# Hybrid S5/HGRN2 block: output projection operands made beside the gating products, norm factors in columns, and four reorderings

## The chip, the cores and the metric

The kernel runs on one core of one Trainium2 chip. A core has TensorE (PE, with its weight loads shown as PEld), VectorE (DVE), ScalarE (ACT), GpSimd (POOL) and SyncE (SP), whose queue issues nearly all DMAs here. The metric is the device time of one execution in microseconds; the median of the runs counts.

## The reference, cut to what matters

One layer over 1024 tokens of width 1024, all in float32:

```python
h = h + 0.5 * swiglu(rmsnorm(h, ffn1_norm), w_gate, w_up, w_down)    # d_ff 2816
u = rmsnorm(h, mix_norm)
s5_in, q, f, i, g, gate_a, gate_b = split_columns(u @ w_in)
y_a = (gelu(s5(s5_in)) @ glu_val) * sigmoid(gelu(s5(s5_in)) @ glu_gate)
o = head_rmsnorm(hgrn2(q, f, i), out_norm) * silu(g)                 # 8 heads of 128
y_b = o @ hg_w_out
h = h + (sigmoid(gate_a) * y_a + sigmoid(gate_b) * y_b) @ w_merge_out
h = h + 0.5 * swiglu(rmsnorm(h, ffn2_norm), ...)
h = h + sigmoid(rmsnorm(h, ple_norm) @ ple_w_gate) * (p @ ple_w_proj)
return rmsnorm(h, final_norm)
```

## The kernel before, in words

Activations are kept transposed: 8 blocks of 128 channels, two halves (h = 0, 1) of 512 tokens, in the tile `r1` (the program's name r). Every large product is taken in three passes of fp32r: each operand is split into a high part (ScalarE, L98 for weights, L345 for activations) and a low part, a subtraction (L99, L346) on VectorE or GpSimd. `mm3` (L354) issues the three passes; a plain unit `proj` is 24 matmuls of 128x512. PSUM has eight buffers of 128x512, the temporaries `t` are eight buffers, the split weights lie in seven slots, the raw weights in four.

Larger products use a seven-product scheme: from the four quarters of the input the sums s1 to s4 are made (`operands`, L452 to L461), from the weights t1 to t4 (`begin`, L119, on VectorE), and each of the seven products is 12 matmuls. `pair` does this for two 128-column blocks of the gates (gg, ga, gb) and of the HGRN2 output projection ("out"); `strassen` does it in the ffns, for 18 of the 22 column blocks, numbers 4 to 21. The split operands lie in the quarters `q0` to `q6`.

Work that is not a matmul is put between matmuls by hand. `self.queue` and `self.scan` are lists of steps; after every fourth matmul `tick` takes one entry from each. An integer n uses up n ticks, a string is a mark that uses one. `flush` runs a queue up to a mark at once. `after(n, f)` runs f when n more `mm3` calls (or steps of the down projection) are through. Beyond that a scheduler orders each engine's instructions at build time: those that it takes to be ready go first, in order of tracing. `paced`, `issue_after` and `keep_in_program_order` add edges to it that fix an order on one engine. Each engine then runs its list in order.

The stages, with their place in the profiled span: ffn1's gate and up products (19 to 477 us), its down projection in seven products of 11 steps (477 to 689, L718), the mixer's S5 input and the first two gate blocks (689 to 757), the other gates as pairs (757 to about 1000), eight HGRN2 heads (to 1453), the S5 gating products `glu` (to 1573, with the last head's steps inside), the output projection (to 1666), the merge, ffn2, and the embedding with the final norm.

What the change touches:

- `norm_rs`: the sum over channels of the squares, by one matmul with ones (L394), then the reciprocal root as eleven VectorE operations on 128x512 (`rsqrt_mean`, L372 to L378). It is called seven times: once in ffn1, twice before the mixer, twice in the merge, twice after ffn2. The final norm (`final`, L1593 and L1605) does it in another form: columns, eleven small operations, diagonals, and matmuls that spread them.
- `s5_params` prepares the S5 parameters on VectorE in 13 pieces. `jobs` calls it (`go`) once in each block of ffn1 from block 5 on, beside its own loads and subtractions (L598) for the down projection. ffn2 has no such pieces.
- `hg_steps(j)`: a head's steps. `gate` loads the stored gate; seven levels (L1207 on TensorE) need the head's k (L1167 on VectorE); transposition, state, output and `back` follow, 34 ticks in all.
- `glu_load` and `glu_split` (L1444, L1445): the S5 output is loaded into eight temporaries and split into q2 and q3, where the mixer's input lay. The last head's f projection is done with h = 1 first so that q2 and q3 come free.
- `glu`: 16 units of 24 matmuls. `mid` runs after the thirteenth: it ends the last head, makes the operands of the output projection and queues the rest.
- `merge`: after the last pair, `mixed` splits the mixed activations, and h is reloaded (L1500) into the rows of r1 that the splits have read. The pairs' `out` loads side_gb (L1484) and the gated S5 part (L1485).

## Time and profile before

| | us |
|---|---|
| median of 3 runs (lowest, highest) | 2557.45 (2555.87, 2560.57) |
| the profiled execution's own time | 2556.42 |
| its span, first to last instruction | 2554.6 |

| engine | busy us | share |
|---|---|---|
| PE | 2449.2 | 96% |
| PEld | 2053.6 | 80% |
| DVE | 1945.9 | 76% |
| ACT | 899.5 | 35% |
| POOL | 885.4 | 35% |

The mean granted TensorE clock is 0.98 of full speed. Times in the rows are microseconds from the span's start. Busy time of PE includes the pipelined tail of each matmul, so a pause shorter than that tail is not seen as idle.

### The profile page before, as it was taken

Reading aid. Unit: us, or ns where it says so; the run is one execution under the profiler, and the core shown is the slowest. Engines: PE = TensorE matmul, PEld = TensorE weight load, DVE = VectorE, ACT = ScalarE, POOL = GpSimd, SP = SyncE. Lnnn points to the kernel's source line nnn. Section 1 sums busy time; section 2 is a strip of 40 time slices with the busy share of each in tenths; the row PEclk is TensorE's granted clock in tenths of the full one; section 3 lists DMA queues with packets and bytes.
Section 4 is the critical chain, followed back from the end, with each engine's and each line's share of the span. In section 5 each row is a group of like instructions: output and inputs, shape, how many; then the busy total and the mean of one; then the engine's idle time right before and its main releaser. Section 6 shows DMA issues by size and latency. Waiting matters only on the chain. (4 is left out here: it accounts for less than half of the span.)

```text
span 2554.6 us, 33785 instructions
## 1 busy us (share of the span) xinstructions
PE 2449.2 (96%) x12030; PEld 2053.6 (80%) x12030; DVE 1945.9 (76%) x2997; ACT 899.5 (35%) x1586; POOL 885.4 (35%) x604
## 2 busy tenths in 40 slices
PE   9999999999999999999999897989999999999996
PEld 7887777788878788989989785878888888788886
DVE  8999999657788775685785557936989999657757
ACT  4322322445534343213213323323332232445533
POOL 3345555200137454112011116652245555200153
PEclk9999999999999999999999998999999999999998
DMA  4255665867423344313312433452246655766212
GB/s 153 91 196 173 207 206 176 287 222 227 147 63 115 124 147 146 81 46 77 86 50 59 137 100 103 152 166 75 83 173 209 228 199 200 272 227 208 86 58 91
DMA packets 195369, 373.29 MB, mean 146 GB/s; under 512 B 34912, under 2 KB 49504, under 8 KB 195168
## 3 DMA queue, kind: packets, MB, share of 16 engines
q1 hardware_dynamic: 194512, 370.57, 44.2%
q8 instruction: 95, 1.56, 0.3%
q14 instruction: 74, 0.61, 0.1%
q10 hardware_dynamic: 688, 0.55, 0.1%
HBM read 257.48 MB, written 113.57 MB: 145 GB/s over the span
## 5 line engine op out<-in xcount | busy, mean ns | idle before, releaser
L354 PE MATMUL mm<-q,wsplit 128*128 128x512 f32 (+1 forms) x7452 | 1705.2, 388 | 50.4 <-ACT q L345 27.5
L354 PEld LDWEIGHTS mm<-q,wsplit 128*128 128x128 f32 x7452 | 1379.4, 190 | 347.0 <-ACT q L345 31.1
L99 POOL TENSOR_TENSOR wsplit<-wraw,wsplit 128x512 fp32r<-128x512 f32 x368 | 536.5, 1472 | 1100.3 <-PE mm L718 386.9
L718 PE MATMUL mm<-wsplit 128*128 128x512 f32 x1848 | 424.0, 392 | 7.4 <-ACT wsplit L345 4.1
L718 PEld LDWEIGHTS mm<-wsplit 128*128 128x128 f32 x1848 | 348.9, 189 | 82.1 <-ACT wsplit L345 5.0
L98 ACT ACTIVATE wsplit<-wraw 128x512 fp32r<-128x512 f32 x464 | 279.8, 624 | 375.0 <-PE mm L354 171.6
L346 DVE TENSOR_TENSOR wsplit<-space,wsplit 128x512 fp32r<-128x512 f32 x308 | 207.8, 712 | 122.7 <-PE mm L718 86.3
L345 ACT ACTIVATE wsplit<-space 128x512 fp32r<-128x512 f32 x308 | 192.4, 631 | 206.2 <-PE mm L718 165.8
L119 DVE TENSOR_TENSOR wraw<-wraw 128x512 f32<-128x512 f32 x153 | 148.0, 968 | 38.5 <-POOL wsplit L99 34.5
L545 DVE TENSOR_TENSOR t<-t,mm 128x512 f32<-128x512 f32 x252 | 167.9, 676 | 0.0
L99 POOL TENSOR_TENSOR wsplit<-t,wsplit 128x512 fp32r<-128x512 f32 x51 | 86.2, 1690 | 211.9 <-ACT wsplit L98 189.9
L598 DVE TENSOR_TENSOR r<-r 128x512 f32<-128x512 f32 x120 | 146.5, 1221 | 6.9 <-DMA r<-in_ffn_w_down_dram 6.1
L98 ACT ACTIVATE wsplit<-t 128x512 fp32r<-128x512 f32 x51 | 32.3, 632 | 266.6 <-DVE t L119 226.4
L1207 PEld LDWEIGHTS mm<-space,space 128*128 128x128 f32 x896 | 109.0, 195 | 16.0 <-DVE space L1167 6.6
L1207 PE MATMUL mm<-space,space 128*128 128x64 f32 x896 | 109.5, 275 | 11.5 <-DVE space L1167 8.8
L99 DVE TENSOR_TENSOR wsplit<-wraw,wsplit 128x512 fp32r<-128x512 f32 x96 | 114.8, 1201 | 4.1 <-ACT wsplit L98 2.6
L354 PE MATMUL mm<-wsplit,q 128*128 128x256 f32 x768 | 101.2, 286 | 0.0
L548 ACT ACTIVATE t<-t 128x512 f32<-128x512 f32 x72 | 45.5, 632 | 141.5 <-DVE t L545 141.5
L354 PEld LDWEIGHTS mm<-wsplit,q 128*128 128x128 f32 x768 | 94.4, 191 | 0.1
L515 POOL TENSOR_TENSOR a<-a 128x512 f32<-128x512 f32 x44 | 70.5, 1601 | 62.1 <-DVE a L536 42.8
L1213 DVE TENSOR_TENSOR space<-space 128x512 f32<-128x512 f32 x48 | 35.2, 734 | 71.1 <-PE mm L1207 71.1
L1334 DVE TENSOR_TENSOR t<-t,mm 128x512 f32<-128x512 f32 x105 | 69.6, 677 | 18.6 <-PE mm L354 12.1
(244 smaller groups left out, 2108.2 us busy)
## 6 DMA issues: line engine op xcount, KB each, us to landing
space<-ffn_act SPq DMA_DIRECT2D x154, 256.0 KB, 3.2
ffn_act<-a SPq DMA_DIRECT2D x110, 256.0 KB, 5.6
wraw<-in_ffn_w_gate_dram SPq DMA_DIRECT2D x44, 512.0 KB, 3.3
wraw<-in_ffn_w_up_dram SPq DMA_DIRECT2D x44, 512.0 KB, 4.2
r<-in_ffn_w_down_dram SPq DMA_DIRECT2D x22, 1024.0 KB, 6.2
ffn_sums<-r SPq DMA_DIRECT2D x22, 1024.0 KB, 6.5
wraw<-in_w_in_dram SPq DMA_DIRECT2D x44, 512.0 KB, 3.8
space<-ffn_sums SPq DMA_DIRECT2D x88, 256.0 KB, 2.8
```

The source lines that it names most:

```text
L98: self.nc.scalar.activation(hi, src, AF.Copy)
L99: engine.tensor_tensor(out=lo, in0=src, in1=hi.bitcast(F32), op=ALU.subtract)
L119: sub = lambda out, x, y: v.tensor_tensor(out=out, in0=x, in1=y, op=ALU.subtract)
L345: self.nc.scalar.activation(hi, src, AF.Copy)
L346: lo_engine.tensor_tensor(out=lo, in0=src, in1=hi.bitcast(F32), op=ALU.subtract)
L354: self.last = nc.tensor.matmul(ps, al if p == 2 else ah, bl if p == 1 else bh, start=p == order[0] and i == 0, stop=p == order[2] and i == ...
L515: g.tensor_tensor(out=x[n], in0=x[a], in1=x[b], op=op)
L545: add = lambda out, x, y: v.tensor_tensor(out=out, in0=x, in1=y, op=ALU.add)
L598: v.tensor_tensor(out=room[:, out, :], in0=room[:, x, :], in1=room[:, y, :], op=ALU.subtract)
L718: self.last = nc.tensor.matmul(ps[j], a[:, j * P:(j + 1) * P], b, start=p == 0 and m == 0, stop=p == NP - 1 and m == 2)
L1207: nc.tensor.matmul(ps[:, c * 64:(c + 1) * 64].rearrange("p (b i) -> p b i", i=h), K[:, c * HC:(c + 1) * HC], q3[:, c * cb:(c + 1) * cb, :] ...
L1334: add = lambda o, x, y: nc.vector.tensor_tensor(out=o, in0=x, in1=y, op=ALU.add)
```

## The change

- `norm_rs` multiplies the squares' sums, 128 columns at a time, with one column of ones, so that the sum over channels lies in four columns of 128 tokens (a new small tile `cols`). The eleven operations run on 128x4. One `mm3` later `spread` makes four diagonals (VectorE), multiplies them with ones (four matmuls of 128 columns) and copies the result (ScalarE). The calls after the ffns come one step earlier in two places.
- `operands` does every low part on VectorE, always uses its gap, and ends its sums with a mark. The output projection's operands are queued behind the last head's steps with gaps of three ticks (`switch`); `mid` only ends that queue and adds a12, and s4 follows the units.
- The S5 parameters: in `jobs` a piece in every second block; the others in the first two products of the down projection, at steps 2, 5 and 8.
- In the S5 matrices' scan the first wait is 30 ticks instead of 16, the waits of 5 are 4. A head waits two more ticks between its gate and its first level.
- The first pair (gg, 1) begins with t2, t3, t1 and takes b11 fourth; its product is added to three sums then.
- The last head: S5 output loaded before its projections, then q and f for h = 1, the splits, q and f for h = 0.
- The reloads of h in the merge are kept behind what is traced on SP before them.

```diff
@@ -232,6 +232,7 @@
...
         nc.vector.memset(self.ones, 1.0)
         self.rs = c.tile([P, 2, HALF], F32, name="rs")
+        self.cols = c.tile([P, 2, 3, 4], F32, name="cols")
         self.gain = {}
@@ -387,12 +388,26 @@
             nc.scalar.activation(sq, self.hsrc(j, h), AF.Square)
             (engine or nc.gpsimd).tensor_tensor(out=accs[h], in0=accs[h], in1=sq, op=ALU.add)
-    def norm_rs(self, h, acc, out=None):
+    def norm_rs(self, h, acc):
+        nc = self.nc
         ps = self.aux()
         with self.tc.issue_after(self.last.ins):
-            self.nc.tensor.matmul(ps, self.ones, acc, start=True, stop=True)
-        self.rsqrt_mean(self.rs[:, h, :], ps, D)
+            for c in range(4):
+                nc.tensor.matmul(ps[:, c:c + 1], acc[:, c * P:(c + 1) * P], self.ones[:, 0:1], start=True, stop=True)
+        cols = iter([self.cols[:, h, i, :] for i in range(3)])
+        col = next(cols)
+        self.rsqrt_mean(col, ps[:, 0:4], D, lambda: next(cols))
+        def spread():
+            ps = self.aux()
+            for c in range(4):
+                dg = self.t()[:, 0:P]
+                nc.vector.tensor_scalar(out=dg, in0=self.ident, scalar1=col[:, c:c + 1], scalar2=None, op0=ALU.mult)
+                with self.tc.issue_after(self.last.ins):
+                    nc.tensor.matmul(ps[:, c * P:(c + 1) * P], self.ones, dg, start=True, stop=True)
+            nc.scalar.activation(self.rs[:, h, :], ps, AF.Copy)
+        self.after(1, spread)
     def norm_x(self, j, h, gain):
@@ -438,7 +453,6 @@
         v = self.nc.vector
-        g = v if gain else self.nc.gpsimd
         A11, A22, A12, S4, S1, S2, S3 = roles
@@ -452,16 +466,16 @@
...
             v.tensor_tensor(out=s1, in0=x21, in1=x22, op=ALU.add)
             v.tensor_tensor(out=s2, in0=s1, in1=x11, op=ALU.subtract)
-            self.split(self.quarter(S3, k), s3, g)
+            self.split(self.quarter(S3, k), s3, v)
             if early:
...
             else:
                 self.split(self.quarter(S1, k), s1, v)
-            self.split(self.quarter(S2, k), s2, g)
+            self.split(self.quarter(S2, k), s2, v)
             v.tensor_tensor(out=s4, in0=x12, in1=s2, op=ALU.subtract)
         def plain(q, j, h):
-            self.split(self.quarter(q, j % 4), self.hsrc(j, h), (v, g)[j % 2])
+            self.split(self.quarter(q, j % 4), self.hsrc(j, h), v)
         def chain(work, gap=0):
@@ -469,7 +483,7 @@
...
             return r
         return dict(
-            sums=chain(sums, gap if gain else 0),
+            sums=chain(sums, gap) + ["sums"],
             s1=chain(lambda k: plain(S1, k, 0)) + ["s1"],
@@ -612,14 +626,14 @@
...
             other = aside(Arena(self.r1[:, 12:16, :].rearrange("p a b -> p (a b)"))) if aside else iter(())
             go = lambda: next(other, None)
+            rest_of.append(go)
             for n in range(NP + 4):
                 do = [lambda n=n, i=i: work(n, i) for i in range(4)]
                 start = [lambda n=n: end(n - 1), 1] if n else []
-                yield start + [do[0], 3, do[1], 2, go, 2, do[2], lambda n=n: begin(n + 2), 2, do[3]]
+                yield start + [do[0], 3, do[1], 2, go if n % 2 else 1, 2, do[2], lambda n=n: begin(n + 2), 2, do[3]]
             yield [lambda: end(NP + 3)]
-            assert next(other, None) is None
         steps = [(i, p) for i in range(7) for p in range(NP)]
-        parts, ring = {}, {}
+        parts, ring, rest_of = {}, {}, []
         def load_s(n):
@@ -729,6 +743,11 @@
...
             load_s(n + 6)
             load_w(n + 6)
+            if i < 2 and p % 3 == 2:
+                rest_of[0]()
+            if (i, p) == (1, NP - 1):
+                for _ in range(8):
+                    rest_of[0]()
             if p == NP - 4 and i in (0, 1, 2, 5):
@@ -1004,10 +1023,10 @@
...
         part = [self.s5_mats(early, b) for b in range(8)]
         go = lambda it: lambda: next(it, None)
-        first = [kept, go(part[0]), 16]
+        first = [kept, go(part[0]), 30]
         for b in range(8):
-            first += [go(part[b]), 5, go(part[b]), 10, go(part[b])]
-            first += [go(part[b + 1]), 5] if b < 7 else []
+            first += [go(part[b]), 4, go(part[b]), 10, go(part[b])]
+            first += [go(part[b + 1]), 4] if b < 7 else []
         def fetch(src, b):
@@ -1307,7 +1326,7 @@
...
             for h in range(2):
                 nc.sync.dma_start(out=self.ho[:, h, :], in_=self.sg[j, h])
-        return [gate] + steps
+        return [gate, 2] + steps
     def mixer_plan(self):
@@ -1326,37 +1345,55 @@
         o += [(("mrg", j), io["w_merge_out"][j]) for j in range(8)]
         self.w.plan(o, self.nc.gpsimd)
-    def pair(self, key, out, refill=None, late=None):
+    def pair(self, key, out, refill=None, late=None, last=False):
         nc, w = self.nc, self.w
         add = lambda o, x, y: nc.vector.tensor_tensor(out=o, in0=x, in1=y, op=ALU.add)
         p1, p16, p167, up = self.t(), self.t(), self.t(), self.t()
-        self.flush("a11")
-        nc.scalar.activation(p1, self.product(key, "b11", "a11"), AF.Copy)
-        add(p16, p1, self.product(key, "t2", "s2"))
-        w.release(key, "b11")
-        add(p167, p16, self.product(key, "t3", "s3"))
-        w.release(key, "t2")
-        if late:
-            late()
-        p5 = self.product(key, "t1", "s1")
-        w.release(key, "t3")
-        add(up, p167, p5)
-        out(1, 0, up)
-        add(p16, p16, p5)
+        if last:
+            self.flush("sums")
+            nc.scalar.activation(p16, self.product(key, "t2", "s2"), AF.Copy)
+            add(p167, p16, self.product(key, "t3", "s3"))
+            w.release(key, "t2")
+            p5 = self.product(key, "t1", "s1")
+            w.release(key, "t3")
+            add(up, p167, p5)
+            add(p16, p16, p5)
+            self.flush("a11")
+            ps = self.product(key, "b11", "a11")
+            w.release(key, "b11")
+            for x in (up, p167, p16):
+                add(x, x, ps)
+            nc.scalar.activation(p1, ps, AF.Copy)
+            out(1, 0, up)
+        else:
+            self.flush("a11")
+            nc.scalar.activation(p1, self.product(key, "b11", "a11"), AF.Copy)
+            add(p16, p1, self.product(key, "t2", "s2"))
+            w.release(key, "b11")
+            add(p167, p16, self.product(key, "t3", "s3"))
+            w.release(key, "t2")
+            if late:
+                late()
+            p5 = self.product(key, "t1", "s1")
+            w.release(key, "t3")
+            add(up, p167, p5)
+            out(1, 0, up)
+            add(p16, p16, p5)
         steps = [("t4", "a22", p167, 0, 0), ("b21", "a12", p1, 0, 1), ("b22", "s4", p16, 1, 1)]
-        last = "t1"
+        used = "t1"
         for piece, q, acc, unit, h in steps[2:] + steps[:2] if refill else steps:
             self.flush(q)
             add(acc, acc, self.product(key, piece, q))
-            w.release(key, last)
-            last = piece
+            w.release(key, used)
+            used = piece
             out(unit, h, acc)
             if q == "s4" and refill:
                 refill()
-        w.release(key, last)
+        w.release(key, used)
     def refill(self):
@@ -1394,23 +1431,28 @@
...
             for p in range(n == "gg", 4):
                 self.pair((n, p), lambda unit, h, z: put(n, 2 * p + unit, h, z),
-                          self.refill if (n, p) == ("gb", 3) else None)
+                          self.refill if (n, p) == ("gb", 3) else None, last=(n, p) == ("gg", 1))
                 if scan:
...
         self.hg_setup(self.arena(4, 5, 6))
         for j in range(HEADS):
-            for key, fn in (("q", self.hg_q), ("f", self.hg_f)):
-                for h in (1, 0) if (key, j) in (("q", 0), ("f", HEADS - 1)) else (0, 1):
-                    fn(j, h)
-                    if (key, j, h) == ("f", HEADS - 1, 1):
+            if j == HEADS - 1:
+                self.scanned()
+                self.glu_load()
+                for h in (1, 0):
+                    self.hg_q(j, h)
+                    self.hg_f(j, h)
+                    if h:
                         self.glu_split(0)
                         self.glu_split(1)
-                w.done((key, j))
-                if key == "q" and j == HEADS - 1:
-                    self.scanned()
-                    self.glu_load()
+                w.done(("q", j), ("f", j))
+            else:
+                for key, fn in (("q", self.hg_q), ("f", self.hg_f)):
+                    for h in (1, 0) if (key, j) == ("q", 0) else (0, 1):
+                        fn(j, h)
+                    w.done((key, j))
             if j % 2 == 0:
@@ -1421,7 +1463,6 @@
...
                 w.done(("va", j // 2), ("vb", j // 2))
         self.glu()
-        self.flush()
         return self.merge()
@@ -1461,15 +1502,20 @@
             v.tensor_tensor(out=s, in0=s, in1=sa, op=ALU.mult)
             nc.sync.dma_start(out=self.ma[j, h], in_=s)
+        ops = {}
+        def switch():
+            self.fresh(4, 5, 6)
+            ops.update(self.operands(None, roles=(0, 6, 2, 3, 5, 1, 4), gap=3))
+            self.queue[0:0] = ops["sums"] + ops["a11"] + ops["a22"]
         def mid():
-            self.flush()
-            self.fresh(4, 5, 6)
-            ops = self.operands(None, roles=(0, 6, 2, 3, 5, 1, 4))
-            late.append(ops["s4"])
-            self.queue = ops["a11"] + ops["sums"] + ops["a22"] + ops["a12"]
-        late = []
+            self.flush("switch")
+            self.queue += ops["a12"]
+        self.queue += [switch, "switch"]
         self.units(unit, "glu", first=2, last=3, mid=mid)
-        self.queue += late[0]
+        self.queue += ops["s4"]
     def glu_x(self, j, h):
@@ -1497,7 +1543,7 @@
...
         for j in range(8):
             for h in range(2):
-                nc.sync.dma_start(out=self.hsrc(j, h), in_=self.hd[j, h])
+                self.tc.keep_in_program_order(nc.sync.dma_start(out=self.hsrc(j, h), in_=self.hd[j, h]))
         accs = [None, None]
@@ -1717,9 +1763,9 @@
...
                 b.after(delay[h], lambda: b.norm_rs(h, acc))
         return each
-    b.ffn("ffn1", "ffn1_norm", lambda j, h: io["x"][j, :, h * HALF:(h + 1) * HALF], finish("mix_norm", True, (2, 3)), aside=b.s5_params)
+    b.ffn("ffn1", "ffn1_norm", lambda j, h: io["x"][j, :, h * HALF:(h + 1) * HALF], finish("mix_norm", True, (2, 2)), aside=b.s5_params)
     b.mixer()
-    b.ffn("ffn2", "ffn2_norm", lambda j, h: b.hd[j, h], finish("ple_norm", False, (2, 4)), b.ple_embedding)
+    b.ffn("ffn2", "ffn2_norm", lambda j, h: b.hd[j, h], finish("ple_norm", False, (2, 3)), b.ple_embedding)
     b.ple()
```

## Rows read from the trace of the kernel before

**Rows 1.** The page, busy time of each engine (share of the span, instructions).

```profile
PE 2449.2 (96%) x12030; PEld 2053.6 (80%) x12030; DVE 1945.9 (76%) x2997; ACT 899.5 (35%) x1586; POOL 885.4 (35%) x604
```

**Rows 2.** Windows: stretch, length, busy (instructions) by engine, clock, DMA share, GB/s.

```profile
1900.00:2000.00 100.00, 100.00 (x443) 82.84 (x442) 92.48 (x101) 30.44 (x53) 53.71 (x36) 1.00 0.65 226
```

**Rows 3.** PE's waits: who for whom, us in total, times, longest.

```profile
PE mm L354 <- ACT q L345: 27.5, 5, 8.0
PE mm L1605 <- DVE t L1604: 9.6, 4, 4.7
PE mm L354 <- ACT wsplit L98: 9.1, 9, 2.2
PE mm L1207 <- DVE space L1167: 8.8, 3, 3.2
...
PE mm L354 <- ACT q L1444: 6.1, 3, 4.0
...
PE mm L944 <- DVE r L939: 4.3, 1, 4.3
```

**Rows 4.** Windows around four waits, columns as in rows 2.

```profile
753.00:770.00 17.00, 11.07 (x28) 6.62 (x27) 13.92 (x14) 11.56 (x21) 12.59 (x9) 0.72 0.33 95
1449.00:1462.00 13.00, 6.93 (x20) 4.66 (x20) 11.95 (x19) 12.95 (x23) 3.17 (x2) 0.79 0.36 112
1573.00:1597.00 24.00, 8.86 (x27) 6.01 (x28) 24.00 (x17) 12.86 (x24) 22.71 (x15) 0.64 0.37 120
1665.00:1680.00 15.00, 6.88 (x21) 4.75 (x20) 11.73 (x13) 6.05 (x11) 9.19 (x6) 0.66 0.60 200
```

**Rows 5.** Windows of the blocks 5 to 21, ffn1 then ffn2.

```profile
137.84:463.75 325.91, 316.61 (x1365) 255.32 (x1364) 308.29 (x526) 93.97 (x179) 169.64 (x112) 0.99 0.58 196
1875.41:2179.68 304.27, 304.27 (x1345) 252.00 (x1344) 276.96 (x300) 91.18 (x161) 168.98 (x112) 1.00 0.60 208
```

**Rows 6.** Window in ffn1's down projection, second product.

```profile
508.00:538.00 30.00, 30.00 (x134) 24.86 (x133) 16.70 (x26) 14.01 (x23) 0.00 (x0) 1.00 0.79 269
```

**Rows 7.** Timeline of DVE, a norm's chain: start, us, engine, line, operation.

```profile
706.35 0.69 DVE L372 TENSOR_SCALAR t<-mm 128x512 f32<-128x512 f32 x1 [5.22 <-PE mm L394]
...
717.15 1.66 DVE L378 SCALAR_TENSOR_TENSOR rs<-t,rs 128x512 f32<-128x512 f32 x1
```

**Rows 8.** Timeline of DVE, the final norm's chain: first and what follows it.

```profile
2544.22 0.16 DVE L372 TENSOR_SCALAR space<-mm 128x2 f32<-128x2 f32 x1 [1.11 <-PE mm L1593]
...
2546.39 0.48 DVE L1604 TENSOR_SCALAR t<-ident,space 128x128 f32<-128x128 f32 x2
```

**Rows 9.** Timeline of PE: a norm's matmul, and the final norm's two.

```profile
705.29 1.02 PE L394 MATMUL mm<-a,ones 128*128 128x512 f32 x2
...
2496.03 0.95 PE L1593 MATMUL mm<-ones,space 128*128 128x1 f32 x8
...
2502.30 1.16 PE L1605 MATMUL mm<-t,ones 128*128 128x128 f32 x8 [1.99 <-DVE t L1604]
```

**Rows 10.** Lines of DVE, 1553.5 to 1597: busy, mean ns, idle.

```profile
L346 DVE TENSOR_TENSOR q<-r,q 128x512 fp32r<-128x512 f32 x6 | 9.9, 1668 | 0.0
```

**Rows 11.** The page's costliest groups: busy, mean ns, idle before and its releaser.

```profile
L99 POOL TENSOR_TENSOR wsplit<-wraw,wsplit 128x512 fp32r<-128x512 f32 x368 | 536.5, 1472 | 1100.3 <-PE mm L718 386.9
...
L346 DVE TENSOR_TENSOR wsplit<-space,wsplit 128x512 fp32r<-128x512 f32 x308 | 207.8, 712 | 122.7 <-PE mm L718 86.3
```

**Rows 12.** Window in the gating products, the last head's steps inside.

```profile
1462.00:1552.00 90.00, 90.00 (x482) 77.18 (x481) 41.93 (x80) 15.94 (x27) 13.09 (x10) 0.99 0.30 101
```

**Rows 13.** Instructions of line L1444: duration ns (least, median, most), first and last.

```profile
L1444 ACT ACTIVATE q<-t x16: 639/650/719, 1449.2 to 1460.4; 128x256 fp32r<-128x256 f32 x16
```

**Rows 14.** Timelines of SP and DVE at the end of the output projection.

```profile
1653.01 6.44 SPq L1500 DMA_DIRECT2D r<-h_spill  x3
...
1664.37 1.38 SPq L1484 DMA_DIRECT2D t<-side_gb  x3
...
1667.66 0.69 DVE L1486 TENSOR_TENSOR t<-t 128x512 f32<-128x512 f32 x1 [3.65 <-DMA t<-side_gb]
```

## Prediction

> **What bounds the kernel now.** TensorE. The page's busy line comes first: PE is busy 96% of the span, VectorE 76%, the rest about a third [rows 1]. So time is won only where PE stands still or runs at its lower clock, or where it gets more or less to do. Its pace when nothing disturbs it is 443 matmuls in 100 us at full clock, 0.2257 us each [rows 2]; a stretch with fewer has lost the difference, whether as an idle gap, as half clock (a granted clock of 0.5 is 1.2 GHz of 2.4) or as a bubble too short to be listed. PE's waits, second, say where: operand splits on ScalarE (L345) 27.5 us, weight pieces (L98) 9.1, the first levels of heads (L1167) 8.8, the splits for the gating products (L1444) 6.1, one transposition (L939) 4.3 [rows 3]. Third, windows around four of these waits, counted at the pace. 753 to 770: 28 matmuls are worth 6.3 us, 10.7 are lost. 1449 to 1462: 20 are 4.5, 8.5 lost. 1573 to 1597: 27 are 6.1, 17.9 lost. 1665 to 1680: 21 are 4.7, 10.3 lost. The granted clock there is 0.64 to 0.79, so the losses hold gap and clock together [rows 4]. Fourth, the 16 transformed blocks of ffn1 against those of ffn2, from the first-product copy of block 5 to that of block 21: same matmuls, 325.91 us against 304.27. ffn1 has 526 DVE instructions to ffn2's 300 and 31 us more DVE time [rows 5]; the 226 more are the S5 parameters, which only ffn1 carries. So they cost PE 21.6 us, though PE's listed waits on weight pieces are only 9.1.
>
> **The sum, part by part**, against the profiled execution's own 2556.4 us (1.0 under the median of the runs, 1.8 over its span).
>
> *S5 parameters.* Thirteen pieces ran in thirteen blocks in a row. Now the first seven go to every second block, and six to the first two products of the down projection. Counted in the code, some 143 of the 226 instructions stay, about 20 of 31 us, spread over seven pairs of blocks: 2.8 us a pair. ffn2's DVE leaves 27.3 us free in its 304 [rows 5], 3.4 a pair. On average it fits; the exponentials, larger than the mean, do not. The moved 11 us go under a stage where DVE has 16.7 of 30 us and POOL nothing, while PE runs at its pace (134 in 30) [rows 6]: free there, and without that slack they would cost their 11. Bounds: 8 (loss in proportion to the instructions that stay) to 18 (nearly all recovered). I take 12, between the two. **-12.**
>
> *First pair of the gates.* a11's splits came late because DVE was. The pair now begins with t2, t3, t1, whose operands are ready earlier, so a11 has three products (36 matmuls, 8.1 us) more, against a loss of 10.7 that holds gap and clock. Ahead of it the norm chain for the second half, eleven 128x512 operations from 706.35 to 718.8 with others in between [rows 7], shrinks to eleven small ones, 2.2 us [rows 8]. What is late next is t1's weight piece, now third instead of fourth: of 10.7 I leave 1.5. **-9** (3 to 10.5).
>
> *Norm factors.* PE did one 128x512 fp32 matmul with ones, two instructions, 1.02 us. Now it does four of one column and four of 128 columns. The final norm has this form already: its eight instructions with one column keep PE 0.95 us, its eight with 128 columns 1.16 [rows 9]. The extra is 0.95 + 1.16 - 1.02 = 1.1 us; seven calls: **+8**. The spread matmuls wait for DVE's four diagonals, with whatever matmul is queued behind them: 2.0 us in the first such wait, 4.7 in the longest [rows 3, 9]. Those had 256-column work and the finished block's scaling beside them; here a whole projection lies between. Bounds nothing and 2 each, I take 0.55: **+4**. DVE's gain elsewhere than at the first pair buys nothing, since PE waits on no norm there.
>
> Against this stands a rule of the Trainium skill (TensorE: Matmul & The Clock Gate, Back-to-back issue gap): a matmul of up to 64 columns issues in about 25 ns. By it the eight would take 0.2 us, the seven norms 5 us less, and the total would be 2508. The rows disagree, with 0.95 for eight, and the sum goes by the rows.
>
> *Operands of the output projection.* Before, they were made in one burst three units before the end of the gating products. DVE took 1.67 us mean for a 128x512 subtraction there [rows 10], against 0.71 in the page's mean of the same line [rows 11], while POOL did its own share at 1.5 [rows 11]. Now everything is on DVE and begins when the last head is done, with three ticks between groups. Work: 4 groups of 7 plus 8 plain splits, 36 operations at 0.7, 25 us. The stage has 96 ticks, one for each four of its matmuls, 0.9 us; the last head's steps take 36 of them, so 53 us are left; the stage's own DVE work is 42 of 90 us, most of it the last head's [rows 12], two operations a unit after it, 14 us. 25 + 14 of 53 fits; at 1.67 a piece it would be 60 + 14 and would not. POOL, only 13 of 90 us busy there [rows 12], is why I take the first. Two splits of four still come at and after the end, with six products before the last is needed. Of 17.9 I leave 1. **-17** (8 to 18).
>
> *Last head.* f's second half was followed by 24 matmuls while 16 splits of 0.65 us ran on ScalarE [rows 13], 10.4 us. Now q and f of the first half follow: 48 matmuls, 10.9 us, and the first gating unit needs only the first eight splits. Late next: the raw sums take all eight temporaries a projection earlier, so head 6's squares and outputs wait for the splits, and its transpositions sit in PE's queue ahead of gating matmuls. I leave 1.5 of 8.5. **-7** (3 to 8.5).
>
> *Reloads in program order.* At 1653 the reloads of h entered SP's queue ahead of the last side loads. They waited there for splits to be done with their rows; the side loads issued at 1664.4, and DVE waited for one until 1667.66 [rows 14]. PE got its operand at 1673.85, 8 us late. Pinned behind, the reloads can hold only themselves and the merge weights queued behind them; the merge's adds wait for them instead, with eight PSUM banks (43 us of units) in hand. The last product's adds and splits, about 3 us, have 5.4 us of products before them. I leave 2.3 of 10.3. **-8** (3 to 10).
>
> *Head steps.* Two ticks before a head's first level are 8 matmuls, 1.8 us, in the two heads that waited 8.8 in all [rows 3]: 3.6. The odd heads run out of ticks two earlier, so their transposition falls into the forced end of the queue: 1 back. **-2.5** (8 gained to 2 lost).
>
> *S5 matrices.* The blocks repeat every 22 instead of 24 ticks and start 14 later; one of them made PE wait 4.3 us [rows 3]. The new phase can remove that wait or make another: **0** (4.3 either way). The earlier norm calls, the extra queue marks and POOL's subtractions of ffn lie under PE's full pace: nothing.
>
> Sum: -12 - 9 + 8 + 4 - 17 - 7 - 8 - 2.5 = -43.5, so 2556.4 - 43.5 = **2513 us**.
>
> **Rivals.** *The operands do not hide.* If DVE runs at its slow duration in the gating stage too, the 17 us stay lost: 2530. For it, that DVE's slow operations come wherever POOL's weight pieces run; against it, POOL's 13 of 90 us. 0.22. *The rest goes too.* The parameters' whole 21.6 us, the spreads without a wait, no left-overs: 9.6 + 4 + 6.3 more, 2493. For it speaks ffn2, which loses nothing with DVE nine tenths busy. 0.15. *The spreads stall PE: slower.* Each norm puts eight instructions into PE's order that wait for DVE; with 55.5 us of gains over seven norms this decides beyond 7.9 us a norm. Waits of 6 us, 1.1 of work and 2 lost at half clock (0.66 over 15 us in [rows 4] is 5 at most) make 64 in place of 12: 2565. The longest wait seen, 4.7, would just about make no change. For it, DVE is nine tenths busy beside the ffn's products [rows 2]; against it, the waits seen are 2.0 and at most 4.7 [rows 3, 9]. 0.05. *The waits only move on*, each recovered gap lost at the next late operand: 2556, 0.03. Forecast 0.55, with 2502 to 2524 of its own.
>
> What a measurement of this kernel tells from no change is about 0.2%, 5 us. Faster 0.92, same 0.03, slower 0.05. The range 2494 to 2534 holds the forecast, the first rival and most of the second.
>
> **What would show it.** In the changed profile: the 16 blocks of ffn1 near 312 us, with parameter lines in the down projection and PE at its pace there; no L345 wait at the end of the gating products, DVE's operand lines beginning about 35 us into them at 0.7 us each; side loads ahead of all h reloads on SP; L1444 gone from PE's waits; eight one-column and eight 128-column instructions per norm, and waits on the diagonals below 2 us. I am wrong if those waits are several us, if glu's matmuls stall on PSUM because DVE lags by more than four units, or if the head 6 transpositions hold PE.

## The result, and the profile after

The changed kernel takes 2530.55 us (median of 4 runs, 2528.49 to 2531.73), the kernel before 2557.94 on the same chip (2555.87 to 2560.57): ratio 0.9891, interval 0.9874 to 0.9909, so 27.4 us or 1.1% faster. The forecast was 2513, its range 2494 to 2534. The direction was right; of the 43.5 us expected 27.4 came. The time lies in the range, but not in the 2502 to 2524 that the prediction gave its own forecast. The profiled execution took 2530.26 us, its span is 2528.1.

Where they came is read off exactly by counting matmuls. Both traces hold 10,212 matmuls (8364 + 1848) on the two lines of the products and the down projections (L354 and L718 before, L355 and L732 after). The start of the n-th in the trace before, less the start of the n-th in the trace after, is what was gained up to there; the difference between two such numbers is what a stretch gained. I call this "by matmul count". Nothing is left over: the rows add up to 26.5, and the spans differ by as much.

| matmuls | stretch | gained, us | the prediction's terms |
|---|---|---|---|
| 0 to 500 | start, first norm | 1.5 | nothing |
| 500 to 2000 | gate/up products of ffn1 | 2.8 | parameters 12 |
| 2000 to 3000 | down projection, two norms | -2.1 | norms -12 in all |
| 3000 to 3300 | first pair of the gates | 9.5 | 9 |
| 3300 to 3700 | S5 matrices | 0.3 | 0 |
| 3700 to 5500 | heads | 0.2 | 2.5 |
| 5500 to 5900 | last head | -3.4 | 7 |
| 5900 to 6200 | end of the gating products, output projection | 20.4 | 17 |
| 6200 to 6500 | end of the output projection | 6.3 | 8 |
| 6500 to 6900 | merge, two norms | -6.2 | (norms) |
| 6900 to 9300 | ffn2 | 0.9 | nothing |
| 9300 to end | two norms, tail | -3.7 | (norms) |

Two rows miss by about 10 us each: the parameters and the last head. The rest stands within 4 of its term. How far to trust a row: each count comes from one profiled execution of a kernel. Runs below that leave the gate/up products alone differ from the changed kernel there by up to 2.8 us, so the 2.8 of that row cannot be told from nothing; in the heads they differ by up to 3.7, and at the start by up to 3.0. Elsewhere unedited stretches mostly agree within 1 us, the others within 1.6, and within 2.9 in e4.

The page of the changed kernel, busy time of each engine, against [rows 1]: PE 4 us less, DVE 43 less.

```profile
PE 2445.2 (97%) x12128; PEld 2062.2 (82%) x12128; DVE 1902.9 (75%) x3043; ACT 908.4 (36%) x1594; POOL 854.8 (34%) x588
```

PE's waits in the changed kernel (who for whom, us, times, longest), against [rows 3]. The operand splits (L346, formerly L345) fell from 27.5 to 3.2 us. The splits of the raw sums are gone from the list, and in their place stands a wait of head 6's transpositions (L1315), 9.2 us in one piece. The weight pieces (L98) fell only from 9.1 to 7.8. The first levels of heads (L1186, formerly L1167) fell from 8.8 to 5.2, but the later levels (L1233, formerly L1214), 2.5 before, rose to 6.8. New are the waits for the diagonals (L408).

```profile
...
PE mm L1315 <- DVE t L1301: 9.2, 1, 9.2
PE mm L355 <- ACT wsplit L98: 7.8, 3, 3.7
...
PE mm L1226 <- DVE space L1233: 6.8, 10, 2.3
PE mm L1226 <- DVE space L1186: 5.2, 2, 3.3
PE mm L408 <- DVE t L406: 4.5, 3, 2.8
PE mm L963 <- DVE r L958: 4.0, 1, 4.0
...
PE mm L355 <- ACT q L346: 3.2, 2, 2.1
```

*The parameters.* Windows of the changed kernel, columns as in [rows 2]: the 16 blocks of ffn1, the block with the longest stall, and the first pair (the 17 us of the first row of [rows 4], where 28 matmuls ran).

```profile
136.18:460.91 324.73, 315.64 (x1361) 258.11 (x1361) 303.60 (x526) 94.99 (x179) 170.88 (x112) 0.98 0.57 197
423.07:445.50 22.43, 17.59 (x70) 13.82 (x69) 21.02 (x55) 5.74 (x11) 10.53 (x8) 0.92 0.54 200
753.00:770.00 17.00, 15.71 (x69) 12.36 (x68) 14.18 (x17) 9.35 (x18) 10.58 (x7) 1.00 0.30 94
```

The 16 blocks take 324.7 us after 325.9, where 312 were expected, and DVE runs 526 instructions in them, exactly as many as before [rows 5]. Not one of the 226 parameter instructions has left. By matmul count 9.5 us had been won in this stretch at matmul 1500 (370 us), and 9.1 were lost again by matmul 1800 (449 us), where the last pieces run. A line of their complex products (L813), its duration in ns and its first and last start:

```profile
L813 DVE TENSOR_TENSOR r<-r x8: 180/206/1318, 370.5 to 419.6; 128x32 f32<-128x32 f32 x8
L813 DVE TENSOR_TENSOR chr<-chr,r x7: 161/164/172, 422.4 to 430.1; 128x16 f32<-128x16 f32 x7
```

The last one starts at 430.1, though it stands in the code among the matmuls of the down projection, the first of which starts at 473.1. What came of it, in the timeline of the changed kernel (start, us, engine, line): the last parameter instruction (L923), only then DVE's differences for a weight piece (L119), ScalarE's split of it (L98), and PE, 3.68 us late.

```profile
430.45 0.23 DVE L923 TENSOR_SCALAR chj<-chj 128x128 f32<-128x128 f32 x1
430.59 0.68 DVE L559 TENSOR_TENSOR t<-t,mm 128x512 f32<-128x512 f32 x1
431.19 0.68 DVE L119 TENSOR_TENSOR t<-wraw 128x512 f32<-128x512 f32 x1
431.91 1.42 DVE L119 TENSOR_TENSOR wraw<-wraw 128x512 f32<-128x512 f32 x2
...
433.42 1.15 ACT L98 ACTIVATE wsplit<-wraw 128x512 fp32r<-128x512 f32 x2 [0.80 <-DVE wraw L119]
434.10 1.22 PE L355 MATMUL mm<-q,wsplit 128*128 128x512 f32 x2 [3.68 <-ACT wsplit L98]
```

*The last head.* Timeline of the changed kernel again. L1485 and L1486 split the raw sums (high halves on ACT, low on DVE), L1293 squares head 6's output, L373 to L379 are its norm's small steps, L1301 scales it, L1315 transposes it.

```profile
1426.15 0.39 PE L1289 MATMUL mm<-space,space 128*128 128x128 f32 x2
...
1426.81 2.36 ACT L1485 ACTIVATE q<-t 128x256 fp32r<-128x256 f32 x4 [2.47 <-PE mm L355]
...
1432.95 0.60 ACT L1175 ACTIVATE space<-mm 128x512 f32<-128x512 f32 x1 [1.12 <-PE mm L355]
1433.45 1.08 ACT L1293 ACTIVATE t<-mm 128x512 f32<-128x512 f32 x2
...
1435.77 0.16 DVE L373 TENSOR_SCALAR space<-space 128x8 f32<-128x8 f32 x1
1435.83 0.60 DVE L1486 TENSOR_TENSOR q<-t,q 128x256 fp32r<-128x256 f32 x1
1436.34 0.17 DVE L374 TENSOR_SCALAR space<-space 128x8 int32<-128x8 int32 x1
...
1441.12 0.17 DVE L379 SCALAR_TENSOR_TENSOR space<-space 128x8 f32<-128x8 f32 x1
1441.39 1.29 DVE L1301 TENSOR_TENSOR t<-mm,space 128x512 f32<-128x512 f32 x2
1442.14 1.11 PE L1315 MATMUL mm<-ident,t 128*128 128x128 f32 x4 [9.22 <-DVE t L1301]
```

Head 6's products are done at 1426.5, but its squares run only at 1433.45: on ACT they stand behind splits of the raw sums and behind the copy of the next projection (L1175). Then eleven steps of 0.16 us take from 1435.77 to 1441.29, because between them DVE works off subtractions of 0.6 us, which themselves wait for ACT. PE runs at half clock from 1437.6 to 1447.9.

*Norms of the merge.* The same pattern, timeline of the changed kernel:

```profile
1728.24 0.16 DVE L374 TENSOR_SCALAR cols<-cols 128x4 int32<-128x4 int32 x1
...
1732.23 0.15 DVE L377 TENSOR_TENSOR cols<-cols 128x4 f32<-128x4 f32 x1
1732.30 0.73 DVE L417 SCALAR_TENSOR_TENSOR q<-r,gains,q 128x512 fp32r<-128x512 f32 x1
...
1735.62 0.87 DVE L406 TENSOR_SCALAR t<-ident,cols 128x128 f32<-128x128 f32 x4
1735.96 1.16 PE L408 MATMUL mm<-t,ones 128*128 128x128 f32 x8 [2.83 <-DVE t L406]
1736.96 0.95 PE L397 MATMUL mm<-ones,t 128*128 128x1 f32 x8
```

The column chain, 2.2 us when alone [rows 8], here takes over 7, an operand split of 0.73 us in nearly every gap, and PE waits 2.83 us.

*The operands of the output projection.* DVE's lines from 1485 to 1640 us (busy, mean ns, idle), against 1668 ns in [rows 10]:

```profile
L347 DVE TENSOR_TENSOR q<-r,q 128x512 fp32r<-128x512 f32 x21 | 18.7, 939 | 0.0
...
L347 DVE TENSOR_TENSOR q<-t,q 128x512 fp32r<-128x512 f32 x12 | 8.7, 776 | 0.0
```

### The profile page after: what moved, and what is told of

It reads as the page before. It is cut to its first block, busy times and chain, and to the rows that moved or that the text cites. A ratio compares the mean times of both kernels' runs of the same rounds, so it can differ in the third digit from the quotient of the medians.

```text
span 2528.1 us, 34047 instructions
## 1 busy us (share of the span) xinstructions
PE 2445.2 (97%) x12128; PEld 2062.2 (82%) x12128; DVE 1902.9 (75%) x3043; ACT 908.4 (36%) x1594; POOL 854.8 (34%) x588
## 5 line engine op out<-in xcount | busy, mean ns | idle before, releaser
L355 PE MATMUL mm<-q,wsplit 128*128 128x512 f32 (+1 forms) x7452 | 1693.6, 387 | 15.3 <-ACT wsplit L98 7.8
L355 PEld LDWEIGHTS mm<-q,wsplit 128*128 128x128 f32 x7452 | 1379.0, 190 | 299.0 <-ACT wsplit L98 9.9
L732 PE MATMUL mm<-wsplit 128*128 128x512 f32 x1848 | 422.8, 391 | 5.5 <-DVE wsplit L347 3.7
L98 ACT ACTIVATE wsplit<-wraw 128x512 fp32r<-128x512 f32 x464 | 281.5, 626 | 372.2 <-PE mm L355 173.5
L732 PEld LDWEIGHTS mm<-wsplit 128*128 128x128 f32 x1848 | 347.5, 188 | 79.0 <-DVE wsplit L347 4.6
L347 DVE TENSOR_TENSOR wsplit<-space,wsplit 128x512 fp32r<-128x512 f32 x308 | 207.8, 712 | 131.8 <-PE mm L732 93.3
L346 ACT ACTIVATE wsplit<-space 128x512 fp32r<-128x512 f32 x308 | 192.6, 633 | 204.6 <-PE mm L732 168.0
L119 DVE TENSOR_TENSOR wraw<-wraw 128x512 f32<-128x512 f32 x153 | 154.3, 1008 | 48.9 <-POOL wsplit L99 44.9
L98 ACT ACTIVATE wsplit<-t 128x512 fp32r<-128x512 f32 x51 | 32.3, 634 | 233.8 <-DVE t L119 204.4
L355 PE MATMUL mm<-wsplit,q 128*128 128x256 f32 x768 | 100.3, 286 | 0.0
L355 PEld LDWEIGHTS mm<-wsplit,q 128*128 128x128 f32 x768 | 94.2, 191 | 0.1
```

The lines of the kernel that those rows point to most:

```text
L98: self.nc.scalar.activation(hi, src, AF.Copy)
L119: sub = lambda out, x, y: v.tensor_tensor(out=out, in0=x, in1=y, op=ALU.subtract)
L346: self.nc.scalar.activation(hi, src, AF.Copy)
L347: lo_engine.tensor_tensor(out=lo, in0=src, in1=hi.bitcast(F32), op=ALU.subtract)
L355: self.last = nc.tensor.matmul(ps, al if p == 2 else ah, bl if p == 1 else bh, start=p == order[0] and i == 0, stop=p == order[2] and i == ...
L732: self.last = nc.tensor.matmul(ps[j], a[:, j * P:(j + 1) * P], b, start=p == 0 and m == 0, stop=p == NP - 1 and m == 2)
```

## The experiments

Each run stands against the kernel before on the same chip. The ratio is to that kernel, with its 95% interval; the changed kernel's is 0.9891 (0.9874 to 0.9909).

| run | us | before, us | ratio | interval |
|---|---|---|---|---|
| e1 parameters tied | 2525.24 | 2555.21 | 0.9878 | 0.9862 to 0.9895 |
| e2 last head undone | 2526.92 | 2555.21 | 0.9889 | 0.9874 to 0.9903 |
| e3 raw sums later, other buffers | 2525.80 | 2555.21 | 0.9884 | 0.9870 to 0.9899 |
| e4 norm factors undone | 2530.60 | 2555.21 | 0.9900 | 0.9885 to 0.9915 |
| e5 parameters all in the down projection | 2515.65 | 2557.94 | 0.9829 | 0.9813 to 0.9846 |
| e6 first pair undone | 2529.49 | 2557.94 | 0.9887 | 0.9872 to 0.9902 |
| e7 operands in a burst | 2544.10 | 2557.94 | 0.9945 | 0.9930 to 0.9960 |
| e8 combined | 2498.39 | 2557.94 | 0.9765 | 0.9751 to 0.9780 |
| e9 operands partly on POOL | 2535.23 | 2557.87 | 0.9918 | 0.9901 to 0.9934 |
| e10 head ticks undone | 2528.71 | 2557.87 | 0.9889 | 0.9874 to 0.9903 |
| e11 reloads free | 2536.14 | 2557.87 | 0.9919 | 0.9905 to 0.9934 |
| e12 raw sums, other buffers only | 2531.62 | 2560.49 | 0.9886 | 0.9870 to 0.9903 |

Only e5, e7 and e8 have intervals clear of the changed kernel's; edits of a few us drown in them. Each is therefore also read by matmul count against the changed kernel, in the stretch it touches (positive: faster than the changed kernel).

**e1, the six last pieces tied in place.** `paced` ties every instruction that its argument issues behind the instruction standing before it on that engine; the kernel's queue runs its steps through it, the pieces in the down projection were called without it.

```
             if i < 2 and p % 3 == 2:
-                rest_of[0]()
+                self.paced(rest_of[0])
```

> The changed kernel with one edit: the six last pieces of the S5 parameters, issued in the down projection, are tied behind the instruction that stands before them on each engine. Theory: untied, they were pulled forward into the gate/up products (the changed kernel's trace has the last parameter instruction at 430.7 us, before the first matmul of the down projection at 473.1), and there DVE made the weight pieces late: the blocks of products from 380.5 and from 423.1 us lost 4.0 and 7.0 us. Tied, the instructions run among the matmuls of the down projection, these two blocks lose under 1 us each, and the total falls by 8 to 11 us, to 2520 to 2523. Rival: in the down projection PE waits for DVE's splits instead, and the total stays at 2528 to 2533. Second rival: the waits have nothing to do with the parameters: the two blocks lose as much as before, 2530.

L813 now runs on to 525.9 us, and DVE's instructions in the 16 blocks fall from 526 to 443 (windows and line of this run):

```profile
136.91:454.18 317.27, 313.99 (x1367) 255.20 (x1367) 295.42 (x443) 91.49 (x163) 169.48 (x112) 1.00 0.58 199
```

```profile
L813 DVE TENSOR_TENSOR r<-r x8: 192/211/221, 372.0 to 496.0; 128x32 f32<-128x32 f32 x8
L813 DVE TENSOR_TENSOR chr<-chr,r x7: 168/169/170, 509.8 to 525.9; 128x16 f32<-128x16 f32 x7
```

The stretch of the products gains 6.0 us, twice what unedited runs differ by there; the stretch with the down projection loses 0.0. The blocks from 380.5 and from 420.1 lose under 1 us each. The theory holds in place and sign; the size is under the 8 to 11 expected. The 83 instructions that left are as many as the prediction had counted to leave (226 - 143). The wait at 308 us, in blocks that the edit leaves alone, stays.

**e5, all pieces but the first in the down projection, tied**, except the last two, which are issued together at the end of the second product, as the code of the changed kernel does with what is left.

```
-                yield start + [do[0], 3, do[1], 2, go if n % 2 else 1, 2, do[2], ...
+                yield start + [do[0], 3, do[1], 2, go if n == 1 else 1, 2, do[2], ...
...
-            if i < 2 and p % 3 == 2:
-                rest_of[0]()
+            if i < 2 and p % 2 == 1:
+                self.paced(rest_of[0])
```

> The changed kernel with all pieces of the S5 parameters but the first in the down projection, each tied behind what stands before it. Theory: the gate/up products lose 16.6 us in ffn1 because DVE has no room beside them, at whatever rhythm the pieces come; the down projection has room (in the first experiment its pieces there cost 0.01 us by matmul count). The 16 blocks then take ffn2's 304 to 306 us in place of 324.7, the down projection gains nothing, and the total is 2512 to 2516. Rival: thirteen pieces in two products of the down projection are too many; DVE's splits for it come late, and 5 to 10 us of the gain are lost there: 2518 to 2524.

Windows of this run, the 16 blocks and 30 us of the down projection:

```profile
137.31:442.00 304.69, 304.69 (x1346) 252.29 (x1345) 276.89 (x302) 91.16 (x160) 168.94 (x112) 1.00 0.61 208
490.00:520.00 30.00, 29.72 (x132) 24.16 (x131) 29.53 (x140) 17.80 (x42) 0.00 (x0) 1.00 0.84 270
```

The blocks now take ffn2's time [rows 5], with no stall. The stretch gains 19.7 us; the down projection gives 0.9 back, with DVE busy 29.5 of 30 us there, where it was 16.7 [rows 6]. The median is 14.9 us under the changed kernel's; the kernel before stood at 2557.94 beside both. It is less than 19.7 because this run's trace also lost 3.7 in the heads, which the edit leaves alone, and 1.1 ahead of matmul 500. The theory holds.

**e2, the order of the last head undone.** The loop over q and f is the old one again, the raw sums loaded behind q.

```
-            if j == HEADS - 1:
-                self.scanned()
-                self.glu_load()
-                for h in (1, 0):
-                    self.hg_q(j, h)
-                    self.hg_f(j, h)
...
+            for key, fn in (("q", self.hg_q), ("f", self.hg_f)):
+                for h in (1, 0) if (key, j) in (("q", 0), ("f", HEADS - 1)) else (0, 1):
+                    fn(j, h)
...
```

> The changed kernel with only the order of the last head undone (q of both halves, then f of both, raw sums loaded behind q). Theory: the new order loses more than it wins, because head 6's transpositions now wait 9.2 us at 1442 us, with half clock behind them; by matmul count it is 3.4 us behind the old order between the first and the second half of the last head. Undone, that wait goes, the wait for the splits of the raw sums (6.1 us in the kernel before) comes back: about 2527. Rival: the 9.2 us come from something else that the change moved (the two ticks ahead of each head): then both waits are there, 2537 to 2540.

The last head gains 3.6 us, the theory's 3.4. The 9.2 us wait is gone; two waits for the splits of the raw sums, 1.5 and 3.8 us with half clock over 6.8 us, are back. The two ticks are still there, so they are not the cause of the 9.2 us.

**e3, four raw sums in the feed-forward's ring, all asked for behind f.**

```
-                self.glu_load()
                 for h in (1, 0):
                     self.hg_q(j, h)
                     self.hg_f(j, h)
                     if h:
+                        self.glu_load()
                         self.glu_split(0)
...
-            raw = self.t(), self.t()
+            raw = (self.a(), self.a()) if j < 2 else (self.t(), self.t())
```

> The changed kernel with the raw sums in other buffers: four of the eight in the ring that the feed-forward uses, the other four in temporaries, all asked for after f of the first half instead of before q. Order of the last head as changed. Theory: head 6's squares and outputs waited because the eight temporaries held raw sums; with four free they run right behind the products that feed them, the 9.2 us wait falls under 2 and its half clock with it: 9 to 12 us less, 2518 to 2521. Rival: the loads now come too late for the first gating unit, which then waits for its splits as in the kernel before (6 us): 2526 to 2532. If the temporaries are not the cause the wait stays at 9 us and the total at 2530.

The last head gains 6.6 us, fewer than the 9 to 12 expected. ACT's timeline in this run: the squares stand right behind the product's end, and the transpositions wait 0.6 us. What stays are 2.2 us of waits for the second four sums, which are loaded late; the rival had put them at 6.

```profile
1426.49 0.60 ACT L1293 ACTIVATE t<-mm 128x512 f32<-128x512 f32 x1 [0.25 <-PE mm L1291]
1428.47 0.60 ACT L1293 ACTIVATE t<-mm 128x512 f32<-128x512 f32 x1 [1.39 <-PE mm L1289]
```

**e12, the buffers of e3 alone**, the sums asked for as early as in the changed kernel.

```
-            raw = self.t(), self.t()
+            raw = (self.a(), self.a()) if j < 2 else (self.t(), self.t())
```

> The changed kernel with one half of the third experiment's edit: four of the eight raw sums in the feed-forward's ring, asked for as early as in the changed kernel. Theory A: the eight temporaries were the cause; with four of them free the squares run behind the products that feed them, and the 9.2 us wait at the transpositions falls under 2: 2521 to 2524. Theory B: not the room but the place where the sums are asked for decides; asked for early, the splits stand ahead of the squares on ScalarE and between the norm's steps on VectorE whatever buffer they read, so the wait stays at 8 to 9 us and the total at 2529 to 2532.

The wait is 9.2 us as before, and ACT's order that of the changed kernel, though four temporaries are now free:

```profile
1425.82 2.36 ACT L1485 ACTIVATE q<-a 128x256 fp32r<-128x256 f32 x4 [2.47 <-PE mm L355]
...
1431.96 0.60 ACT L1175 ACTIVATE space<-mm 128x512 f32<-128x512 f32 x1 [1.13 <-PE mm L355]
1432.46 1.08 ACT L1293 ACTIVATE t<-mm 128x512 f32<-128x512 f32 x2
```

So theory A falls: room in the temporaries is not enough by itself. Since e3 differs from this run only in the place where the sums are asked for, that place is needed. Whether it is enough with all eight in the temporaries was not tried.

**e4, the norm factors undone**, with the delays that go with them.

```
     def norm_rs(self, h, acc):
...
         ps = self.aux()
         with self.tc.issue_after(self.last.ins):
-            for c in range(4):
...
+            self.nc.tensor.matmul(ps, self.ones, acc, start=True, stop=True)
+        self.rsqrt_mean(self.rs[:, h, :], ps, D)
...
```

> The changed kernel with only the norm factors as before: one matmul of 128x512 with ones, eleven operations of 128x512 on DVE, no spreading. Theory: by matmul count the column form cost 12.3 us over seven norms, and the first pair's 9.5 us came from beginning with t2, t3 and t1; so undoing it wins 10 to 12: 2518 to 2521. Rival: the first pair's gain came from the short chain on DVE ahead of it; then undoing gives back 6 to 9 of the 12: 2524 to 2528.

The theory falls. The rival was right about the cause: the first pair loses 9.1 us again, though it still begins with t2, t3 and t1. On the other side the norms of the mix win 2.0, those of the merge 6.2, those behind ffn2 3.3 (matmuls 9300 to 9600). The total, 2530.60, lies above both ranges: this trace also loses 2.2 to 2.6 us each before its first matmul, at the end of the output projection and in ffn2, and wins 2.9 in the S5 matrices; no run shows why. The window of the first pair in this run, where 20 us at the pace would hold 88 matmuls:

```profile
755.00:775.00 20.00, 15.88 (x55) 11.05 (x54) 18.41 (x17) 12.32 (x24) 13.57 (x9) 0.82 0.28 105
```

**e6, the first pair in its old order**, columns kept.

```
-                          ..., last=(n, p) == ("gg", 1))
+                          ..., last=False)
```

> The changed kernel with the first pair in its old order (a11's product first), the norm factors in columns as changed. Theory after the fourth experiment: the short chain on DVE makes a11's splits early enough by itself; the wait is 1 to 3 us and the total at 2528 to 2532. Rival: both are needed, the order as well: then the pair loses 6 to 9 us again, 2534 to 2538.

The pair's stretch changes by 0.0 us: in the 17 us of its window 69 matmuls run, as in the changed kernel.

```profile
751.30:768.30 17.00, 15.71 (x69) 12.36 (x68) 14.18 (x17) 9.27 (x18) 10.52 (x7) 1.00 0.29 94
```

So the whole 9.5 come from the norm factors, of which the short chain on DVE is the part ahead of this pair; the new order adds nothing that this count can see. The second half's norm is also called one step earlier in the changed kernel, e4 undoes that with the rest, and no run takes the two apart.

**e7, the operands in the old burst, all on DVE.**

```
...
         def mid():
-            self.flush("switch")
-            self.queue += ops["a12"]
+            self.flush()
+            self.fresh(4, 5, 6)
+            ops = self.operands(None, roles=(0, 6, 2, 3, 5, 1, 4))
+            late.append(ops["s4"])
+            self.queue = ops["a11"] + ops["sums"][:-1] + ops["a22"] + ops["a12"]
...
```

> The changed kernel with the operands of the output projection in one burst three units before the end of the gating products, as before, but all on DVE. Theory: the place is what counts; 36 operations of 0.7 us and more do not fit into three units, and 14 to 20 us come back: 2544 to 2550. Rival: what made the burst slow was POOL's share of it; all on DVE it is done in 25 us, and 4 to 8 us come back: 2534 to 2538.

Of the 26.7 us of the two stretches (matmuls 5900 to 6500) 12.8 are lost again (10.1 and 2.7), a little under the theory's 14 to 20 and over the rival's 4 to 8. The rest stays won without the new place. The waits for the operands' splits are 10.8 us in place of 3.2:

```profile
PE mm L355 <- ACT q L346: 10.8, 3, 4.9
```

**e9, the new place, 16 low halves on POOL again.**

```
+        g = v if gain else self.nc.gpsimd
...
-            self.split(self.quarter(S3, k), s3, v)
+            self.split(self.quarter(S3, k), s3, g)
...
-            self.split(self.quarter(q, j % 4), self.hsrc(j, h), v)
+            self.split(self.quarter(q, j % 4), self.hsrc(j, h), (v, g)[j % 2])
```

> The changed kernel with the operands of the output projection made where the change puts them, but 16 of their 36 low halves on POOL again, as before. The burst all on DVE gave back 13 us. Theory: the place is what counts, and beside the gating products POOL has time for 16 operations of 1.7 us (it is busy 18 of 110 us up to 1552 us): within 2 us of 2530. Rival: with POOL at work DVE's operations take 1.7 us in place of 0.7 and POOL's weight pieces come late: 5 to 10 us more, 2535 to 2541.

By matmul count 3.0 us are lost, all at one wait at the end of the output projection (5.0 us in place of 2.1). DVE's own subtractions (L347), 939 ns before, take 1431 ns while POOL does its share:

```profile
L347 DVE TENSOR_TENSOR q<-r,q 128x512 fp32r<-128x512 f32 x13 | 18.2, 1431 | 0.0
```

The runs spread from 2530 to 2538, so between the 3 us of the count and the 7 of the ratio the price stays open; the sign agrees with the rival's. The Trainium skill (Perfetto Trace Analysis, Optimizing Scalar/DVE Operations) says that GpSimd and VectorE share a read port of SBUF, so that moving work between the two may not help; the two means agree with that.

**e10, no ticks ahead of the heads' steps.**

```
-        return [gate, 2] + steps
+        return [gate] + steps
```

> The changed kernel without the two ticks ahead of each head's steps. Theory, after the profile of the changed kernel: what the ticks win at the first level of a head they lose at its forced end (2.9 us at 1237.8 us), since by matmul count the heads of before and after take the same time: within 1.5 us of 2530. Rival (the prediction's term): they win 2.5 us: 2533.

2528.71, ratio 0.9889 against 0.9891: no difference. The heads' stretch gains 1.9 us, less than unedited runs differ there. The waits show an exchange, but more at the later levels than at the forced end that the theory named: without the ticks the first levels (L1186) wait 9.0 us in place of 5.2, the later levels (L1233) 2.5 in place of 6.8, and the forced end (L1256) 1.6 in place of 2.9.

```profile
PE mm L1226 <- DVE space L1186: 9.0, 4, 2.9
...
PE mm L1226 <- DVE space L1233: 2.5, 5, 1.2
```

**e11, the reloads of h not kept in order.**

```
-                self.tc.keep_in_program_order(nc.sync.dma_start(out=self.hsrc(j, h), in_=self.hd[j, h]))
+                nc.sync.dma_start(out=self.hsrc(j, h), in_=self.hd[j, h])
```

> The changed kernel with the reloads of h free to be moved forward again. Theory: the late side loads, not the operands, held the merge: by matmul count the change won 6.2 us there, and undone they come back, 2535 to 2538. Rival: with the operands made earlier the loads no longer collide, and nothing changes: 2530.

3.9 us are lost by matmul count where the change had won 6.3, and the ratio is 0.9919. PE's waits for the operands' splits are 7.0 us in place of 3.2, the longest 6.0. The sign is the theory's. The rest of the 6.3 fits the earlier operands: with them undone (e7) this stretch loses 2.7.

```profile
PE mm L355 <- ACT q L346: 7.0, 2, 6.0
```

**e8, three edits together:** e5's, e3's, and `norm_rs` with a flag by which the norms of the merge and behind ffn2 use one 128x512 matmul and the long chain again (behind ffn2 with the old delay), the others columns.

```
...
+        if wide:
+            with self.tc.issue_after(self.last.ins):
+                nc.tensor.matmul(ps, self.ones, acc, start=True, stop=True)
+            self.rsqrt_mean(self.rs[:, h, :], ps, D)
+            return
...
```

> The changed kernel with three edits together: the parameters in the down projection, the raw sums in other buffers, and the norm factors in columns only up to the first pair (the norms of the merge and behind ffn2 again with 128x512). By matmul count: 14 to 16 from the products, 6.6 from the last head, 3.7 to 6 from the norms: 2502 to 2508. Rival: the gains overlap or move on to the next late operand, and the total is no lower than 2514.

2498.39, ratio 0.9765: 59.6 us under the kernel before and 32.2 under the changed one. By matmul count the parts add up without loss: 19.7 in the products, -1.1 in the down projection, 6.6 in the last head, 6.2 in the merge, 3.3 behind ffn2 (matmuls 9300 to 9600). The rival falls, and the theory's 2502 to 2508 was too high: the products gave more than its 14 to 16, the norms 9.5 in place of 3.7 to 6. The page of this run:

```profile
PE 2433.2 (98%) x12072; PEld 2053.4 (82%) x12072; DVE 1925.1 (77%) x3027; ACT 902.1 (36%) x1590; POOL 854.0 (34%) x588
```

## Why the prediction was right in direction and wrong in size

*Parameters, 12 forecast, 2.8 measured: the step that failed.* "six to the first two products of the down projection" and "some 143 of the 226 instructions stay" were counted in the code. The count was right (e1: 83 leave when tied), but in the changed kernel's trace all 226 stayed: untied, the pieces had been put where their inputs allowed, ahead of the products that they were meant to run beside. The prediction had seen this very mechanism in the reloads, which had slipped ahead of the side loads [rows 14], and did not ask it of the parameters. What it said of the down projection, "free there", was right (e1: 0.0, e5: 0.9 for all), and so was the price of all of them, 21.6 us: 2.8 + 19.7 = 22.5, within what unedited runs differ by.

*Last head, 7 forecast, 3.4 lost: the second step that failed.* The late next operand was named, "head 6's squares and outputs", and priced at 1.5 us, and the prediction has it among its signs of being wrong; it cost 9.2 and a half-clock stretch. The cause given, the eight temporaries, is not enough by itself (e12). What was not seen is that splits asked for early get ahead of head 6's squares and in between its small steps.

*Norms, 12 forecast, 12.0 measured* (2.1 + 6.2 + 3.7, of which the last 0.4 stand behind its norms; the first of the seven lies in the first row and lost 0.3 by matmul 100). The extra instructions have the durations of [rows 9]: eight of one column 0.95 us, eight of 128 columns 1.16. Each of these instructions comes with a 128x128 weight load of its own in the trace. The issue floor that the prediction took from the Trainium skill (TensorE: Matmul & The Clock Gate, Back-to-back issue gap), by which the former would take 0.2 us, does not fit these eight; the same section calls it the gap of an isolated matmul and says that at small sizes it counts no weight load, so it was the wrong figure to hold against the rows. The waits for diagonals are 2.8, 1.0 and 0.6 us, 4.5 in all against 4 forecast, but in three places, the longest over the bound of 2. So the sum came out, and the even 0.55 a norm did not.

*First pair, 9 forecast, 9.5 measured, for half the reason.* The prediction gave the reordering 8.1 us of room and the short chain a sentence. e4 and e6 show that the new norm factors do it without the reordering. A sum that agrees had hidden a wrong share.

*Operands, 17 forecast, 20.4 measured.* The mechanism was right: DVE's subtractions at 0.78 to 0.94 us in place of 1.67, no wait at the end of the gating products. They began later than forecast, at 1508 us, behind the last head, and still were in time. Place and engine both count (e7 12.8, e9 3.0).

*Reloads, 8 forecast, 6.3 measured*, 3.9 of it the edit's alone (e11). Fifteen of the sixteen reloads now stand behind the side loads:

```profile
1630.99 1.37 SPq L1530 DMA_DIRECT2D t<-side_gb  x3
...
1639.17 11.84 SPq L1546 DMA_DIRECT2D r<-h_spill  x15
```

*Head steps, 2.5 forecast, 0.2 measured* (e10: nothing): the first levels fell from 8.8 to 5.2 us, but the later levels rose from 2.5 to 6.8, and the forced transposition (L1256) waits 2.9 where e10 has 1.6. What the prediction gave back, 1 us for the forced transposition alone, was too little. *S5 matrices, 0 and 0.3*: the wait moved from one block to another, 4.0 after 4.3 us.

*The rivals.* The time fell on 2530, the very number of "the operands do not hide", and that did not happen: their wait is gone. Two other terms together failed by 19.6 us, about as much as that rival's 17. The range held the time because it took in this rival, so that it held is luck. "The rest goes too", 2493, was not far off in time: e8 takes 2498, but by taking the columns out of four norms, not by spreads without a wait. The spreads stalled PE by 4.5 us in all, far from the 6 a norm at which that rival turns.

## What to carry to other kernels

Where a framework orders the instructions, a piece of work moved in the code may not move in the trace unless it is tied there; count its instructions in the window of the trace (526 and 526) before its gain is believed. Here a chain of small dependent steps lasted as long as what the scheduler put between them, so price it by its neighbours and not by its own durations. And take a result apart term by term, by the n-th matmul of both traces: here the total sat on a rival's number while that rival's mechanism was absent, and one right term had the wrong cause.

## What the runs showed that was not expected

A chain of eleven small operations, 2.2 us when alone, took 5.5 us in the last head and over 7 in the merge with 0.6 and 0.73 us operations between its steps. DVE can be busy 29.5 of 30 us beside a down projection and cost PE 0.9 us in two products (e5), while in the gate/up products, where it was busy 95% of the window [rows 5], the same work cost 22.5.
